# A two-layer trunk on one core: the odd mixer's output product, the down projections' product order and the opening's mean square rearranged

## The chip, the core and the metric

The kernel runs on one core of a Trainium2 chip. Its time is the device time of one execution in microseconds (us); the lower the better. Five engines work side by side and wait for each other by semaphores: TensorE (PE in the profile; its weight loads PEld), VectorE (DVE), ScalarE (ACT), GpSimd (POOL) and SyncE (SP), which issues transfers.

## The reference

```python
def reference(x, mem, ...):
    h = x
    for i in range(DEPTH):                       # DEPTH 2, SEQ 512, D_MODEL 1024, D_FF 2816
        f = swiglu_ffn(rms_norm(h, ffn1_pre_g[i]), ffn1_w_gu[i], ffn1_w_down[i])
        h = h + 0.5 * rms_norm(f, ffn1_post_g[i])
        hn = rms_norm(h, mix_pre_g[i])
        m = even_mixer(hn, ...) if i % 2 == 0 else odd_mixer(hn, ...)
        h = h + rms_norm(m, mix_post_g[i])
        c = memory_cross_attention(rms_norm(h, xa_pre_g[i]), mem, ...)
        h = h + rms_norm(c, xa_post_g[i])
        f = swiglu_ffn(rms_norm(h, ffn2_pre_g[i]), ffn2_w_gu[i], ffn2_w_down[i])
        h = h + 0.5 * rms_norm(f, ffn2_post_g[i])
    return h

def swiglu_ffn(h, w_gu, w_down):
    gate, up = jnp.split(h @ w_gu, 2, axis=-1)
    return (jax.nn.silu(gate) * up) @ w_down

def odd_mixer(h, w_in, w_group, scale, w_out):
    # p = h @ w_in, in 4 groups of 256 columns; group g: causal mean over WINDOWS[g] = (2, 4, 8, 16)[g]
    # positions, minus p; then (group @ w_group[g]) * scale, and the 1024 columns @ w_out
```

## The kernel before

The residual h stays in SBUF, 4 tiles of 128 positions. Every product is made of three matmuls (`mm3`): each operand is split into a high part (ScalarE casts it, line 72) and a low part (VectorE subtracts, line 73), and high by high, high by low and low by high are added up (lines 77, 78, 79). So an operand is ready only when ScalarE and then VectorE have had it; weights too (`whi`, `wlo`, made of a loaded `raw` tile), four of each kind, from seven `raw` tiles that SyncE fills (512 KB each). GpSimd issues transfers that add to what a tile holds already.

A feed-forward block works on its 2816 hidden columns in three parts (`FF_PARTS`). Up and gate of a part are made by `seven`, a scheme in which seven products of half-sized blocks take the place of eight; a product there is 24 matmuls of 256 columns. The hidden values are put into two tiles r, cut in four blocks: r11 and r12 are the left halves (positions 0 to 255), r21 and r22 the right halves. The down projection of the first two parts is made by `seven_tm`, again with seven products (24 matmuls of 512 columns each), in banks A, B and C of PSUM, whose operands are blocks and sums of blocks: a11 is r11, x1 is r21 - r22, x2 is x1 - r11, a12 is r12, x3 is r11 - r21, and so on; the weights are t1, b11, b21, b22, t3 and sums of them. The last half of r is written by line 580, after the last product of `seven`. There are 2 x 2 feed-forward blocks, so 8 passes through `seven_tm`; a first part (`fresh`) copies its results into f, a second part adds to them. The third part is made by `tm_last`, position tile by position tile, with the sandwich norm behind it: f is added (line 524), squared and summed on ScalarE (526), multiplied by the gain (532), m follows (533), GpSimd raises it to the power -1/2 (r, line 156), and line 536 adds to h.

The odd mixer makes its input projection, evacuates each group (`evac`), and VectorE makes the causal means (`pool`, lines 848 to 858). Then each group is multiplied by its weight matrix: two products of six matmuls (512 columns) to a group, evacuated by lines 891 (ScalarE, high) and 892 (VectorE, low). `tm_out` multiplies the result y by w_out: its first part (`head`) does four of eight blocks of rows of w_out, those of groups 3 and 2, for all four position tiles and the first 512 output columns, which is 4 x 4 x 3 = 48 matmuls and a quarter of the whole; then tile by tile the rest.

`rms_transpose` does a norm in front of a block: squares and sums on ScalarE (line 164), m on VectorE (166, 169), r on GpSimd, a scaled copy on ScalarE (173), and TensorE transposes it (180), from where VectorE (182) and `split` make the operands. In the opening this is done for the first two tiles before anything else, while the first weights land.

The tiles come from pools, and a scheduler decides by a model of costs and of free tiles in which order each engine gets its instructions; on each engine they then run in that order.

Of the kernel before, what the change touches and what calls it, by code (L numbers as in the profile page):

```python
# [10 lines left out]
P = 128  # L11
D = 1024
# [21 lines left out]
def trunk_kernel(tc, x, mem, ffn1_pre_g, ffn1_w_gu, ffn1_w_down, ffn1_post_g,  # L34
# [8 lines left out]
    with ExitStack() as es:  # L43
# [115 lines left out]
        def rms_transpose(src, g, x, t):  # L159
            xn = qt([P, D])  # L160
            ss = [small(1, "ss") for _ in range(2)]
            hs = [slice(0, 512), slice(512, 1024)]
            for i in range(2):
                nc.scalar.activation(out=xn[:, hs[i]], in_=src[:, hs[i]], func=AF.Square, accum_out=ss[i])
# [5 lines left out]
                                           op0=ALU.mult, op1=ALU.add)  # L170
            r = rsqrt(m2)
# [16 lines left out]
        class Prenorm:  # L188
# [12 lines left out]
            def tile(self, t):  # L201
                self.turns.append(rms_transpose(h[:, t, :], self.g, self.x, t))
# [131 lines left out]
        def seven_tm(w, k0, r, a11, f, fresh):  # L334
# [20 lines left out]
            b11 = load(0, 0)  # L355
            b22 = load(1, 1)
            b21 = load(1, 0)
            r11, r12, r21, r22 = r[0][:, :, :HALF], r[1][:, :, :HALF], r[0][:, :, HALF:], r[1][:, :, HALF:]

            def operand(src):  # L360
                o = ops4()
                split(o[:, 0], o[:, 1], src)
                return o
# [42 lines left out]
            a12 = operand(r12)  # L406
            u2 = product("A", t1, x2)
            t3 = load(0, 1)
            put(t3, 1, 1)
            put(t1, 1, 0)  # L410
            b22 = load(1, 1)
            take(0, 1, u2, None if fresh else "from")
# [8 lines left out]
            take(1, 0, product("A", t1, a22), None if fresh else add)  # L421
# [19 lines left out]
        def tm_out(a, w, k_order, post_g, nxt):  # L441
# [13 lines left out]
            for k in pairs[2:]:  # L455
                wk.update(w_pair(w, k, 0))
# [45 lines left out]
        def tm_last(a, wk, n, post_g, nxt, f):  # L502
# [3 lines left out]
            for t in range(NT):  # L506
# [12 lines left out]
                for c in range(2):  # L519
# [7 lines left out]
                    if c == 0:  # L527
# [29 lines left out]
        def ffn(pre, w_gu, w_down, post_g, nxt):  # L557
            f = []
            for j0, j1 in FF_PARTS:
# [3 lines left out]
                a11 = None  # L563
                for j in range(j0, j1, 2):
# [24 lines left out]
                    if not ending and j - j0 == 2:  # L589
                        a11 = ops4()  # L590
                        split(a11[:, 0], a11[:, 1], r[0][:, :, :HALF])
                n = j1 - j0
                if ending:
                    nx = nxt()
                    last_weights(w_down, j0, n, wk, False)
                    tm_last(hid, wk, n, post_g, nx, f)
                else:
                    seven_tm(w_down, j0, r, a11, f, not f)
# [223 lines left out]
        def odd(pre, l, o, post_g, nxt):  # L822
# [51 lines left out]
            for half in (1, 0):  # L874
# [4 lines left out]
                for g in (2 * half + 1, 2 * half):  # L879
                    if half == 0:  # L880
                        pool(g)
                    gi = g % 2
                    for j in range(2):
                        ps = psa()
                        for k in range(2):
# [7 lines left out]
                                                       op0=ALU.mult, op1=ALU.subtract)  # L893
            nx = nxt()
# [155 lines left out]
```

## Time and profile before

| | |
|---|---|
| three runs | 1979.59, 1980.74, 1982.03 us (median 1980.74) |
| profiled execution | 1980.61 us |
| span, first to last instruction | 1978.9 us |
| mean granted TensorE clock | 0.998 |
| TensorE busy | 1941.2 us, 98% |
| weight loads (beside the matmuls) | 1780.1 us, 90% |
| VectorE busy | 1480.1 us, 75% |
| ScalarE busy | 1036.0 us, 52% |
| GpSimd busy | 216.2 us, 11% |

The busy time of an engine is the time in which it ran an instruction; the profiled execution's own time is 1.7 us more than its span. The granted clock is 1.00 at 2.4 GHz and 0.50 at 1.2 GHz.

### The profile page before, as it was taken

Reading aid. Unit: us, or ns where it says so; the run is one execution under the profiler, and the core shown is the slowest. Engines: PE = TensorE matmul, PEld = TensorE weight load, DVE = VectorE, ACT = ScalarE, POOL = GpSimd, SP = SyncE. Lnnn points to the kernel's source line nnn. Section 1 sums busy time; section 2 is a strip of 40 time slices with the busy share of each in tenths; the row PEclk is TensorE's granted clock in tenths of the full one; section 3 lists DMA queues with packets and bytes.
Section 4 is the critical chain, followed back from the end, with each engine's and each line's share of the span. In section 5 each row is a group of like instructions: output and inputs, shape, how many; then the busy total and the mean of one; then the engine's idle time right before and its main releaser. Section 6 shows DMA issues by size and latency. Waiting matters only on the chain. (4 is left out here: it accounts for less than half of the span.)

```text
span 1978.9 us, 31832 instructions
## 1 busy us (share of the span) xinstructions
PE 1941.2 (98%) x12843; PEld 1780.1 (90%) x12843; DVE 1480.1 (75%) x1840; ACT 1036.0 (52%) x1477; POOL 216.2 (11%) x225
## 2 busy tenths in 40 slices
PE   7999999999999999999999999999999999999998
PEld 7989899888989889899998989899979889999897
DVE  6787877699956568877877786887766648776974
ACT  6555455544565455555455555455545545555462
POOL 1111110100010011111101111110001001111100
PEclk9999999999999999999999999999999999999999
DMA  7887884325845337888871787885234325887871
GB/s 203 223 213 185 202 206 154 109 86 181 280 143 185 86 75 182 213 181 203 212 214 43 203 206 190 201 211 173 75 107 147 98 57 129 208 215 199 203 184 43
DMA packets 251149, 327.76 MB, mean 166 GB/s; under 512 B 9854, under 2 KB 189654, under 8 KB 248954
## 3 DMA queue, kind: packets, MB, share of 16 engines
q1 hardware_dynamic: 193226, 241.80, 38.7%
q0 software_dynamic: 57600, 83.90, 23.3%
q8 instruction: 100, 1.64, 0.3%
q14 instruction: 47, 0.39, 0.1%
q10 hardware_dynamic: 176, 0.05, 0.0%
HBM read 315.22 MB, written 10.49 MB: 165 GB/s over the span
## 5 line engine op out<-in xcount | busy, mean ns | idle before, releaser
L77 PE MATMUL psa<-big,whi 128*128 128x256 f32 (+1 forms) x3056 | 883.1, 290 | 3.1 <-ACT big L72 3.1
L78 PE MATMUL psa<-big,whi 128*128 128x256 f32 (+1 forms) x3056 | 884.6, 290 | 0.5 <-DVE big L73 0.5
L79 PE MATMUL psa<-big,wlo 128*128 128x256 f32 (+1 forms) x3056 | 882.6, 289 | 0.5 <-DVE wlo L73 0.5
L72 ACT CAST whi<-raw 128x1024 fp32r<-128x1024 f32 x514 | 537.9, 1050 | 585.3 <-PE psa L78 260.0
L73 DVE TENSOR_TENSOR wlo<-raw,whi 128x1024 fp32r<-128x1024 f32 x514 | 625.3, 1224 | 238.5 <-ACT whi L72 235.8
L77 PEld LDWEIGHTS psa<-big,whi 128*128 128x128 f32 x3056 | 585.2, 192 | 12.1 <-ACT big L72 4.6
L78 PEld LDWEIGHTS psa<-big,whi 128*128 128x128 f32 x3056 | 586.0, 192 | 9.0 <-DVE big L73 1.4
L79 PEld LDWEIGHTS psa<-big,wlo 128*128 128x128 f32 x3056 | 585.5, 192 | 7.7 <-DVE wlo L73 0.7
L77 PE MATMUL psa<-whi,big 128*128 128x512 f32 x800 | 314.7, 393 | 7.7 <-ACT big L72 6.2
L78 PE MATMUL psa<-wlo,big 128*128 128x512 f32 x800 | 312.0, 390 | 0.0
L79 PE MATMUL psa<-whi,big 128*128 128x512 f32 x800 | 311.2, 392 | 0.4
L77 PEld LDWEIGHTS psa<-whi,big 128*128 128x128 f32 x800 | 150.6, 188 | 41.1 <-ACT big L72 9.5
L79 PEld LDWEIGHTS psa<-whi,big 128*128 128x128 f32 x800 | 150.3, 188 | 37.0 <-DVE big L73 5.6
L78 PEld LDWEIGHTS psa<-wlo,big 128*128 128x128 f32 x800 | 150.5, 188 | 30.1
L300 POOL DMA_DIRECT2D raw<-in_ffn_w_gu_dram x40 | 51.5, 1288 | 571.0 <-DMA raw<-in_ffn_w_gu_dram 428.0
L77 PE MATMUL psa<-big 128*128 128x512 f32 (+1 forms) x288 | 106.1, 370 | 0.8 <-ACT big L72 0.8
L78 PE MATMUL psa<-big 128*128 128x512 f32 (+1 forms) x288 | 105.7, 367 | 0.0
L156 POOL TENSOR_TENSOR r<-m,nhalf 128x1 f32<-128x1 f32 x74 | 47.0, 635 | 536.0 <-DVE m L533 184.7
L79 PE MATMUL psa<-big 128*128 128x512 f32 (+1 forms) x288 | 105.2, 366 | 0.0
L350 POOL DMA_DIRECT2D raw<-in_ffn_w_down_dram x48 | 57.5, 1225 | 261.6 <-DMA raw<-in_ffn_w_down_dram 155.2
L295 POOL DMA_DIRECT2D raw<-in_ffn_w_gu_dram x40 | 52.1, 1303 | 283.3 <-DVE big L73 148.4
L741 DVE SCALAR_TENSOR_TENSOR big<-big,par 128x511 f32<-128x511 f32 (+29 forms) x120 | 81.2, 743 | 0.0
(152 smaller groups left out, 1698.0 us busy)
## 6 DMA issues: line engine op xcount, KB each, us to landing
raw<-in_ffn_w_gu_dram SPq DMA_DIRECT2D x216, 512.0 KB, 4.7
raw<-in_ffn_w_down_dram SPq DMA_DIRECT2D x120, 512.0 KB, 4.2
raw<-in_ffn_w_gu_dram POOLq DMA_DIRECT2D x80, 512.0 KB, 8.1
raw<-in_ffn_w_down_dram POOLq DMA_DIRECT2D x48, 512.0 KB, 7.6
raw<-in_xa_w_kv_dram SPq DMA_DIRECT2D x32, 512.0 KB, 4.1
raw<-in_ev_w_in_dram SPq DMA_DIRECT2D x16, 512.0 KB, 5.3
kv<-big POOLq DMA_DIRECT2D x8, 1024.0 KB, 6.8
raw<-in_xa_w_q_dram SPq DMA_DIRECT2D x16, 512.0 KB, 3.4
```

The costliest lines, as they stand in the source:

```text
L72: nc.scalar.copy(out=hi, in_=src)
L73: nc.vector.tensor_tensor(out=lo, in0=src, in1=hi.bitcast(F32), op=ALU.subtract)
L77: nc.tensor.matmul(out=ps, lhsT=lhs[0], rhs=rhs[0], start=start, stop=skip, skip_group_check=skip)
L78: nc.tensor.matmul(out=ps, lhsT=lhs[0], rhs=rhs[1], start=False, stop=skip, skip_group_check=skip)
L79: nc.tensor.matmul(out=ps, lhsT=lhs[1], rhs=rhs[0], start=False, stop=stop or skip, skip_group_check=skip)
L156: nc.gpsimd.tensor_tensor(out=r, in0=m, in1=nhalf.broadcast_to([P, n]), op=ALU.pow)
L295: nc.gpsimd.dma_start(out=t1, in_=fm_rows(w, 0, ca), accum_op=ALU.add)
L300: nc.gpsimd.dma_start(out=t3, in_=fm_rows(w, 1, cb), accum_op=ALU.add)
L350: nc.gpsimd.dma_start(out=raws[kk], in_=rows(kh, kk, ch), accum_op=ALU.add)
L741: nc.vector.scalar_tensor_tensor(out=acc[:, c, s_:], in0=z[:, c, :SEQ - s_], scalar=par[:, c, CONV - 1 - s_:CONV - s_], in1=acc[:, c, s_:] ...
```

## The change

Four places are rearranged; the products computed are the same, but for the mean square of one tile, which is made from mean and variance.

1. The opening: the mean square of the second position tile is made by VectorE (`mean_square_stats`: two BN_STATS, one BN_AGGR, two small ones) and not by two squares on ScalarE.
2. `seven_tm`: the seven products stand in another order. The first two are p1 (a11) and the one with a12; then u2 (x2), q5 (x1), t3 (x3), and the last two as before. x3 and a11 are made in `ffn` after the second pair of hidden columns (`ready`), r11 - r21 is kept in r11's place, x2 is made from it in one instruction, b21 is loaded before b22, and the sum t1 + b22 goes into b11's tiles.
3. `tm_last`: the multiply by the gain is done by halves of the columns, and m and r stand in front of the second half's.
4. The odd mixer: the groups' products are cut in two (`grouped`). Groups 3 and 2 come first, then `tm_out` begins, and groups 1 and 0 follow behind its head.

```diff
+        def mean_square_stats(src, hs):
+            room = tp.tile([P, 512], F32, name="tmp", tag="tmp")
+            st = room[:, :12].rearrange("p (a b) -> p a b", a=2)
+            for i in range(2):
+                nc.vector.bn_stats(out=st[:, i, :], in_=src[:, hs[i]])
+            mv = room[:, 12:14]
+            nc.vector.bn_aggr(out=mv, in_=st)
+            m = small(1, "m")
+            nc.vector.tensor_scalar(out=m, in0=mv[:, 1:2], scalar1=EPS, scalar2=None, op0=ALU.add)
+            m2 = small(1, "m")
+            nc.vector.scalar_tensor_tensor(out=m2, in0=mv[:, 0:1], scalar=mv[:, 0:1], in1=m,
+                                           op0=ALU.mult, op1=ALU.add)
+            return m2
...
+            m2 = mean_square_stats(src, hs) if stats else mean_square(src, xn, hs)
...
             b11 = load(0, 0)
+            b21 = load(1, 0)
             b22 = load(1, 1)
-            b21 = load(1, 0)
...
-            e = qt([P, 4, HALF])
-            nc.vector.tensor_tensor(out=e, in0=r21, in1=r22, op=sub)
-            x1 = operand(e)
-            p1 = product("A", b11, a11)
+            a12 = operand(r12)
+            p1 = product("A", b11, ready[0])
...
-            nc.vector.tensor_tensor(out=e, in0=e, in1=r11, op=sub)
+            e = qt([P, 4, HALF])
+            nc.vector.scalar_tensor_tensor(out=e, in0=x3r, scalar=-1.0, in1=r22, op0=ALU.mult, op1=sub)
             x2 = operand(e)
+            take(0, 0, product("B", b21, a12), add)
+            for kk in range(2):
+                nc.vector.tensor_tensor(out=b11[kk], in0=t1[kk], in1=b22[kk], op=add)
+            nc.vector.tensor_tensor(out=r21, in0=r21, in1=r22, op=sub)
+            x1 = operand(r21)
+            u2 = product("A", b11, x2)
+            t3 = load(0, 1)
+            put(t3, 1, 1)
+            put(b11, 1, 0)
+            b22 = load(1, 1)
+            take(0, 1, u2, None if fresh else "from")
             q5 = product("C", t1, x1)
-            for kk in range(2):
-                nc.vector.tensor_tensor(out=t1[kk], in0=t1[kk], in1=b22[kk], op=add)
...
-            a12 = operand(r12)
-            u2 = product("A", t1, x2)
...
-            take(0, 0, product("B", b21, a12), add)
-            nc.vector.tensor_tensor(out=r11, in0=r11, in1=r21, op=sub)
-            x3 = operand(r11)
+            x3 = ready[1] if fresh else operand(x3r)
             take(1, 1, product("A", t3, x3), sub)
...
-            for k in pairs[2:]:
-                wk.update(w_pair(w, k, 0))
+            wk.update(w_pair(w, pairs[2], 0))
+            if mid:
+                mid()
+            wk.update(w_pair(w, pairs[3], 0))
...
-                m = small(1, "m")
-                nc.vector.tensor_tensor(out=ft, in0=ft, in1=gb, op=ALU.mult)
-                nc.vector.scalar_tensor_tensor(out=m, in0=ss[1], scalar=4.0 / D, in1=m0,
-                                               op0=ALU.mult, op1=ALU.add)
-                r = rsqrt(m)
+                    else:
+                        m = small(1, "m")
+                        nc.vector.scalar_tensor_tensor(out=m, in0=ss[1], scalar=4.0 / D, in1=m0,
+                                                       op0=ALU.mult, op1=ALU.add)
+                        r = rsqrt(m)
+                    nc.vector.tensor_tensor(out=ft[:, cs], in0=ft[:, cs], in1=gb[:, cs], op=ALU.mult)
...
                     if not ending and j - j0 == 2:
-                        a11 = ops4()
-                        split(a11[:, 0], a11[:, 1], r[0][:, :, :HALF])
+                        r11, r21 = r[0][:, :, :HALF], r[0][:, :, HALF:]
+                        ready = [operand(r11)]
+                        nc.vector.tensor_tensor(out=r11, in0=r11, in1=r21, op=ALU.subtract)
+                        if not f:
+                            ready.append(operand(r11))
...
-            for half in (1, 0):
+            def grouped(half):
...
+            grouped(1)
+            pool(1)
             nx = nxt()
-            tm_out(y, od_w_out[o], [6, 7, 4, 5, 2, 3, 0, 1], post_g, nx)
+            tm_out(y, od_w_out[o], [6, 7, 4, 5, 2, 3, 0, 1], post_g, nx, lambda: grouped(0))
...
-            pre.tile(t)
+            pre.tile(t, stats=t == 1)
```

Lines of the changed kernel have other numbers: 325, 327 and 580 become 344, 346 and 602; 402 becomes 421, the sum into b11; 417 and 422 make x2 and x1; 856 becomes 881; 891 and 892 become 916 and 917; 533 and 536 become 554 and 558.

VectorE at the first down part of the first block (the scheduler numbers the q tiles; in line 73 a `big` is an operand's low half, a `wlo` a weight's). Before:

```order
L325 TENSOR_TENSOR q_943<-q_943,psa 128x2x256
L73 TENSOR_TENSOR wlo<-raw,whi 128x1024
L327 TENSOR_TENSOR q_943<-psa,q_943 128x2x256
L580 TENSOR_TENSOR big<-q_942,q_943 128x2x256
L73 TENSOR_TENSOR wlo<-raw,whi 128x1024
L402 TENSOR_TENSOR raw<-raw 128x1024
L73 TENSOR_TENSOR wlo<-raw,whi 128x1024
L580 TENSOR_TENSOR big<-q_942,q_943 128x2x256
L402 TENSOR_TENSOR raw<-raw 128x1024
L392 TENSOR_TENSOR q_1170<-big 128x1024
L73 TENSOR_TENSOR wlo<-raw,whi 128x1024
L73 TENSOR_TENSOR big<-q_1170,big 128x1024
```

In the changed kernel:

```order
L421 TENSOR_TENSOR raw<-raw 128x1024
L344 TENSOR_TENSOR q_947<-q_947,psa 128x2x256
L73 TENSOR_TENSOR wlo<-raw,whi 128x1024
L346 TENSOR_TENSOR q_947<-psa,q_947 128x2x256
L602 TENSOR_TENSOR big<-q_946,q_947 128x2x256
L73 TENSOR_TENSOR wlo<-raw,whi 128x1024
L421 TENSOR_TENSOR raw<-raw 128x1024
L73 TENSOR_TENSOR big<-big 128x1024
L602 TENSOR_TENSOR big<-q_946,q_947 128x2x256
L73 TENSOR_TENSOR wlo<-raw,whi 128x1024
L417 SCALAR_TENSOR_TENSOR q_1214<-big 128x1024
L422 TENSOR_TENSOR big<-big 128x4x256
```

The last two sums of weights stood around the last hidden half (580), with x1's subtraction (392) behind them; now the first sum (421) stands in front of the third product's addition (344), a12's low half in front of the last hidden half (602), and x2 (417) and x1 (422) behind it.

TensorE in the odd mixer, from the end of groups 3 and 2 on: line 77 to 79 with `big` on the left are a group's product, those with `whi` or `wlo` on the left of `big` are the output product. Before:

```order
L79 MATMUL psa_14581<-big_14543,wlo_14549 128x512
L77 MATMUL psa_14607<-big_14604,whi_14592 128x512
L77 MATMUL psa_14618<-big_14604,whi_14592 128x512
L78 MATMUL psa_14607<-big_14604,whi_14592 128x512
...
L77 MATMUL psa_14636<-big_14633,whi_14592 128x512
L77 MATMUL psa_14645<-big_14633,whi_14592 128x512
L77 MATMUL psa_14657<-whi_14663,big_14559 128x512
L78 MATMUL psa_14657<-wlo_14664,big_14559 128x512
```

In the changed kernel:

```order
L79 MATMUL psa_14593<-big_14555,wlo_14561 128x512
L77 MATMUL psa_14616<-whi_14622,big_14571 128x512
L78 MATMUL psa_14616<-wlo_14623,big_14571 128x512
...
L79 MATMUL psa_14619<-whi_14628,big_14572 128x512
L77 MATMUL psa_14692<-big_14610,whi_14688 128x512
...
L79 MATMUL psa_14703<-big_14610,wlo_14689 128x512
L77 MATMUL psa_14616<-whi_14682,big_14699 128x512
...
L77 MATMUL psa_14721<-big_14718,whi_14688 128x512
```

Before, group 1 (big_14604) and group 0 (big_14633) follow on group 2, and the head (psa_14657 to 14660) begins among them; now the head's 48 matmuls (psa_14616 to 14619) stand between group 2 (psa_14593) and group 1 (psa_14692), and group 0 (psa_14721) comes after the first of what follows the head for tile 0.

VectorE over the same stretch: pool(0) is 848 to 856 before and 873 to 881 now, 892 or 917 evacuate groups' products. Before:

```order
L848 COPY big<-big 128x2
L849 TENSOR_TENSOR big<-big 128x2x511
L892 SCALAR_TENSOR_TENSOR big<-psa,cols,big 128x512 x2
L73 TENSOR_TENSOR big<-q_14596,big 128x1024
L892 SCALAR_TENSOR_TENSOR big<-psa,cols,big 128x512
L854 TENSOR_TENSOR big<-big,rec 128x2
L858 SCALAR_TENSOR_TENSOR big<-big 128x2x511
L892 SCALAR_TENSOR_TENSOR big<-psa,cols,big 128x512 x3
L856 TENSOR_TENSOR big<-big 128x2
L73 TENSOR_TENSOR wlo<-raw,whi 128x1024
L73 TENSOR_TENSOR big<-big 128x1024
```

In the changed kernel:

```order
L917 SCALAR_TENSOR_TENSOR big<-psa,cols,big 128x512 x2
L73 TENSOR_TENSOR big<-q_14602,big 128x1024
L917 SCALAR_TENSOR_TENSOR big<-psa,cols,big 128x512
L73 TENSOR_TENSOR wlo<-raw,whi 128x1024
L917 SCALAR_TENSOR_TENSOR big<-psa,cols,big 128x512
L879 TENSOR_TENSOR big<-big,rec 128x2
L883 SCALAR_TENSOR_TENSOR big<-big 128x2x511
L881 TENSOR_TENSOR big<-big 128x2
L73 TENSOR_TENSOR wlo<-raw,whi 128x1024 x2
L917 SCALAR_TENSOR_TENSOR big<-psa,cols,big 128x512
L73 TENSOR_TENSOR big<-big 128x1024
```

Before, three evacuations stand between 858 and 856 of pool(0); now the three last steps of pool(0) stand together, before the fifth evacuation.

## Rows read from the trace of the kernel before

**Rows 1.** What TensorE waits for, whole span: engine, tile, line, releaser, us, times, longest:
```profile
PE psa L77 <- ACT big L72: 10.1, 12, 2.7
PE tps L180 <- ACT q L173: 7.5, 5, 2.5
```

**Rows 2.** Timeline at the second product of a down part: start us, us, engine, line:
```profile
1719.93 1.22 DVE L402 TENSOR_TENSOR raw<-raw 128x1024 f32<-128x1024 f32 x1
...
1720.22 0.39 PE L79 MATMUL psa<-whi,big 128*128 128x512 f32 x1
...
1721.06 1.22 DVE L392 TENSOR_TENSOR q<-big 128x1024 f32<-128x1024 f32 x1
...
1722.26 0.39 PE L79 MATMUL psa<-whi,big 128*128 128x512 f32 x1
1722.32 1.05 ACT L72 CAST big<-q 128x1024 fp32r<-128x1024 f32 x1 [1.25 <-DVE q L392]
...
1723.41 0.50 PE L77 MATMUL psa<-whi,big 128*128 128x512 f32 x1 [0.77 <-ACT big L72]
...
1725.01 0.40 PE L77 MATMUL psa<-whi,big 128*128 128x512 f32 x1
```

**Rows 3.** What the results of line 392 are waited for by, us and times:
```profile
  ACT big L72: 10.0, 8
```

**Rows 4.** Timeline ahead of the same down part, VectorE and loads:
```profile
1707.96 6.12 SPq L345 DMA_DIRECT2D raw<-in_ffn_w_down_dram  x3
...
1711.53 0.69 DVE L325 TENSOR_TENSOR q<-q,psa 128x512 f32<-128x512 f32 x1 [0.72 <-PE psa L79]
...
1714.34 0.69 DVE L327 TENSOR_TENSOR q<-psa,q 128x512 f32<-128x512 f32 x1 [0.65 <-PE psa L79]
```

**Rows 5.** Loads of the page, last figure the median us from issue to landing:
```profile
raw<-in_ffn_w_down_dram SPq DMA_DIRECT2D x120, 512.0 KB, 4.2
```

**Rows 6.** Loads issued from 1670 to 1677 us, in the same form:
```profile
raw<-in_ffn_w_gu_dram SPq DMA_DIRECT2D x1, 512.0 KB, 6.5
```

**Rows 7.** Timeline of the odd mixer before its groups 0:
```profile
1456.22 1.22 DVE L858 SCALAR_TENSOR_TENSOR big<-big 128x1022 f32<-128x1022 f32 x1
...
1457.83 0.40 PE L79 MATMUL psa<-big,wlo 128*128 128x512 f32 x1
...
1458.98 0.75 DVE L892 SCALAR_TENSOR_TENSOR big<-psa,cols,big 128x512 fp32r<-128x512 f32 x1 [0.22 <-ACT big L891]
1459.65 0.15 DVE L856 TENSOR_TENSOR big<-big 128x2 f32<-128x2 f32 x1
...
1459.84 1.04 ACT L72 CAST big<-big 128x1024 fp32r<-128x1024 f32 x1 [0.89 <-DVE big L856]
...
1460.93 1.22 PE L77 MATMUL psa<-big,whi 128*128 128x512 f32 x2 [2.71 <-ACT big L72]
```

**Rows 8.** Busy time by engine of that stretch, granted clock, DMA share, GB/s:
```profile
1461.00:1464.40 3.40, 3.40 (x8) 2.72 (x9) 3.40 (x3) 1.77 (x2) 0.00 (x0) 0.51 0.49 157
```

**Rows 9.** Timeline of the opening:
```profile
8.45 1.33 ACT L173 ACTIVATE q<-h,r 128x512 f32<-128x512 f32 x2
...
12.05 1.34 ACT L173 ACTIVATE q<-h,r 128x512 f32<-128x512 f32 x2
...
12.83 3.08 PE L180 MATMUL tps<-ident,q 128*128 128x128 f32 x12 [2.50 <-ACT q L173]
...
17.29 0.39 PE L78 MATMUL psa<-big,whi 128*128 128x256 f32 x1 [0.53 <-DVE big L73]
```

**Rows 10.** Statistics instructions of the even mixer, ns min/median/max:
```profile
L679 DVE BATCH_NORM_STATS2 st<-big x4: 682/684/704, 434.0 to 443.8; 128x6 f32<-128x512 f32 x4
```

**Rows 11.** Timeline of the tail:
```profile
1971.87 1.23 DVE L532 TENSOR_TENSOR big<-big,post 128x1024 f32<-128x1024 f32 x1 [0.85 <-ACT sq L526]
1973.02 0.15 DVE L533 SCALAR_TENSOR_TENSOR m<-pss,m 128x1 f32<-128x1 f32 x1
...
1973.83 1.28 DVE L536 SCALAR_TENSOR_TENSOR h<-big,r,h 128x1024 f32<-128x1024 f32 x1 [0.66 <-POOL r L156]
```

More of the change, by code (lines that the diff above doesn't have):

```diff
@@ L157, in rsqrt, with mean_square @@
             return r
-        def rms_transpose(src, g, x, t):
-            xn = qt([P, D])
+        def mean_square(src, junk, hs):
             ss = [small(1, "ss") for _ in range(2)]
-            hs = [slice(0, 512), slice(512, 1024)]
             for i in range(2):
-                nc.scalar.activation(out=xn[:, hs[i]], in_=src[:, hs[i]], func=AF.Square, accum_out=ss[i])
+                nc.scalar.activation(out=junk[:, hs[i]], in_=src[:, hs[i]], func=AF.Square, accum_out=ss[i])
             m = small(1, "m")
@@ L170, in rms_transpose @@
                                            op0=ALU.mult, op1=ALU.add)
+            return m2
[11 more added lines that the diff above has]
+                                           op0=ALU.mult, op1=ALU.add)
+            return m2
+        def rms_transpose(src, g, x, t, stats=False):
+            xn = qt([P, D])
+            hs = [slice(0, 512), slice(512, 1024)]
+            m2 = mean_square_stats(src, hs) if stats else mean_square(src, xn, hs)
             r = rsqrt(m2)
@@ L199, in warm, with tile @@
                 self.ws = sum((w_fm(w, c0, raw) for c0, raw in zip(c0s, raws)), [])
-            def tile(self, t):
-                self.turns.append(rms_transpose(h[:, t, :], self.g, self.x, t))
+            def tile(self, t, stats=False):
+                self.turns.append(rms_transpose(h[:, t, :], self.g, self.x, t, stats))
             def turn_pair(self):
@@ L332, in seven, with operand, seven_tm @@
             done(out_a, out_b, product("A", b11, x.a22, False))
-        def seven_tm(w, k0, r, a11, f, fresh):
+        def operand(src):
+            o = ops4()
+            split(o[:, 0], o[:, 1], src)
+            return o
+        def seven_tm(w, k0, r, ready, f, fresh):
             def rows(kh, kk, ch):
@@ L355, in seven_tm @@
             b11 = load(0, 0)
+            b21 = load(1, 0)
             b22 = load(1, 1)
-            b21 = load(1, 0)
[L358 to L363, printed above, removed]
+            x3r, r12, r21, r22 = r[0][:, :, :HALF], r[1][:, :, :HALF], r[0][:, :, HALF:], r[1][:, :, HALF:]
             banks = {}
@@ L405, in seven_tm @@
             take(1, 1, q5, None if fresh else add)
-            a12 = operand(r12)
-            u2 = product("A", t1, x2)
[L408 to L412, printed above, removed]
-            take(0, 0, product("B", b21, a12), add)
-            nc.vector.tensor_tensor(out=r11, in0=r11, in1=r21, op=sub)
-            x3 = operand(r11)
+            x3 = ready[1] if fresh else operand(x3r)
             take(1, 1, product("A", t3, x3), sub)
@@ L420, in seven_tm @@
             take(0, 1, product("C", b22, x4), "from")
-            take(1, 0, product("A", t1, a22), None if fresh else add)
+            take(1, 0, product("A", b11, a22), None if fresh else add)
         def tm_part(accs, a, w, ks, first, last, ts=range(NT)):
@@ L439, in w_pair, with tm_out @@
             return {(c, k + i): (hi[:, i, :], lo[:, i, :]) for i in range(2)}
-        def tm_out(a, w, k_order, post_g, nxt):
+        def tm_out(a, w, k_order, post_g, nxt, mid=None):
             gb = gain(post_g, "post")
@@ L562, in ffn @@
                 r = None if ending else [big(F32), big(F32)]
-                a11 = None
+                ready = None
                 for j in range(j0, j1, 2):
@@ L597, in ffn @@
                 else:
-                    seven_tm(w_down, j0, r, a11, f, not f)
+                    seven_tm(w_down, j0, r, ready, f, not f)
             return nx
@@ L879, in odd @@
                 for g in (2 * half + 1, 2 * half):
-                    if half == 0:
+                    if g == 0:
                         pool(g)
```

## The prediction

> **What bounds the kernel now.** I read first the waits of TensorE, because TensorE works through nearly the whole span, so a change can only win where TensorE waits or runs at a lower clock. In that list the reader is to see that two kinds of wait hold nearly all: first matmuls that wait for the ScalarE cast of an operand (10.1 us in 12 waits), and transposes that wait for a scaled tile (7.5 us in 5) [rows 1]. Then I looked up where they stand, in the timeline. Eight of the twelve are the same place, the down projection of the first two parts of each feed-forward block (`seven_tm`, two parts in four blocks): VectorE's L392 is what the cast waits for, eight times [rows 3]. The longest one is in the odd mixer, 2.71 us [rows 7], and what follows it runs at a granted clock of 0.51 for 3.4 us [rows 8], which is the 1.2 GHz level. The longest transposes' waits lie in the opening [rows 9]. The tail behind the last matmul is a short chain on VectorE [rows 11].
>
> **The change, part by part.** The sum is made against the profiled execution, 1980.61 us (span 1978.9, and 1.7 around it); the median of the runs is 1980.74, so the two can be taken as one.
>
> *Down parts.* In one site the second product's first matmul should follow the last of p1 by one pitch, 0.227 us (1720.22 to 1722.26 is nine steps). It starts at 1723.41, and the sixth matmul after 1722.26 starts at 1725.01, since x1's low half is late too and the matmuls that want it are spread: 2.75 us for six steps that take 1.36, so 1.39 lost [rows 2]. Eight sites make 11.1. (These rows are from a first part. The profile has four sites of each kind.) The chain that is late is also there: the last half of the hidden tile, then L402, L392, ScalarE's cast from 1722.32 to 1723.37, in one line [rows 2]. The new order puts p1 and B in front, whose operands a11 and a12 come from halves of the hidden tiles that are done before the last one, and makes the first late operand (x2) wanted two products later. A product is 24 matmuls, 24 x 0.227 = 5.44 us, so p1 begins at 1722.26 + 0.23 - 5.44 = 1717.05 and u2 would begin at 1727.93, its first matmul on x2's low half two pitches later, 1728.38. What VectorE has to do after the last hidden half, which ends as L402 starts at 1719.93, by the new program order is at worst L421, a12's low half, one weight low half, L417, L422, another weight low half and x2's: seven at 1.13 (1719.93 to 1721.06), 7.9, so 1727.8: in time by 0.5. In a second part two additions into the output (of L325's kind, 0.69 each [rows 4]) stand between them as well: 1729.2, late by 0.8, at four sites 3.3. At best L421 and a12's half lie ahead of 1719.32, and it is in time everywhere. ScalarE has one cast for each of these operands and is not full there. t3 and the last b11 are loaded, and added to by GpSimd's queue, no later than today, as each waits for a weight tile that is now used no later.
>
> There is one new danger. The first L421 (b11 = t1 + b22) now stands on VectorE in front of L344, the read of bank A that the last `seven` product waits for. L344 is today's L325, at 1711.53; the last product can start when the one before it ends, which the start of L327 shows, 1714.34 [rows 4]. b22 is now loaded after b21, so its first half goes out where b21's does today, at 1707.96 [rows 4], and at the 4.2 us that such a load takes [rows 5] it lands at 1712.2. L421 may begin at 1714.34 - 0.69 - 1.13 = 1712.5 at the latest. So it fits by 0.3 at the median load and doesn't if it takes over 4.5. One load of that size on this queue took 6.5 [rows 6]. I charge 0.1 a site, 0.8 in all, for this and for x2 together. **Term: -10.3; between -5.5 (0.7 lost again at each site) and -11.1**, or -12 if the second parts lose a little more today than the site that I read.
>
> That a late instruction holds up ready ones behind it is what the odd mixer's rows show: L892 at 1458.98 had waited 0.22 for ScalarE, and L856 behind it, whose input was written by L858 (1456.22, 1.22 long), starts at 1459.65 [rows 7]. The Trainium skill (Perfetto Trace Analysis, section Tensor Engine Instruction) says the same of these queues, "ACT/DVE/GPSIMD are strict FIFO". By that rule a late b22 reaches TensorE in full, and the trace agrees.
>
> *Odd mixer.* Today pool(0)'s last step L856 stands behind the evacuations of group 1 on VectorE, ScalarE casts its result at 1459.84, and TensorE, done at 1457.83 with what it could do, starts group 0 at 1460.93: 3.10 less one pitch is 2.87 lost [rows 7]. Half clock for 3.4 us [rows 8] loses 1.7 more. The change puts 48 head matmuls (10.9 us at 0.227) in front of groups 1 and 0. VectorE's work until pool(0) is ready is the same, so with 10.9 us of cover against 2.87 missing it is ready long before. What is late next: the first output matmuls of columns that group 1 and 0 make. Each group product is six matmuls, 1.36, and its evacuation 0.69 on ScalarE and 0.75 on VectorE, of which the first output matmul needs the first and its third the second; counted through, each is in time by 0.2 to 0.4. I leave 0.2 for it. SP's second group load goes behind two output loads, wanted 10.9 us later than before. **Term: -4.4, between -1 and -4.6.**
>
> *Opening.* The second tile's squares leave ScalarE, so its scaling starts where the first tile's ends, 8.45 + 1.33 = 9.78, instead of 12.05: 2.27 earlier [rows 9]. VectorE takes two BN_STATS (0.68 each [rows 10]) and an aggregate instead, ahead of the first weight's low half, where it has little else to do. The transposes' wait of 2.50 shrinks by it. But TensorE waits again, at 17.29, for a low half from VectorE [rows 9], which must come earlier as well, and two later tiles are scaled after that. Of 2.27 I take two thirds, **-1.5, between -0.5 and -2.5** (the whole wait).
>
> *Last part.* m and r no longer stand behind the multiply by the gain. In the tail L533 follows the 1.23 us of L532, 1973.02 against 1971.87, and the last L536 waits for r [rows 11]. So h comes 1.15 earlier: one half of the multiply is done before the last matmul, the other fits between m and h, which are 0.81 apart. **-1.1, between -0.9 and -1.15.** The other fifteen ends of this form have no wait of TensorE that I can price; 0, between +0.5 (0.15 more of VectorE each, if some count) and -0.9.
>
> **Sum:** 10.3 + 4.4 + 1.5 + 1.1 = 17.3, and 1980.6 - 17.3 = **1963.3**.
>
> **The rivals.**
> 1. *The wait moves to b22 or x2* (VectorE's order, above). For it: both margins are some tenths. Against: with a load of median length both are in time. With 0.7 lost a site, 5.6 less the 0.8 charged: 1968.1.
> 2. *The odd mixer pays again.* Four of six banks now hold the output's sums, so the four group products take turns in two, and a bank is free only after 0.69 + 0.75. For it: the two evacuations (1.44) are longer than the next product (1.36). Against: output matmuls can stand between. If a gap near 2.7 comes back, the half clock does too, and the term is gone: 1967.7.
> 3. *The new order brings the down parts nothing*, as x2 is as late as x1 was. For it: it has the same chain of subtraction, cast and subtraction. Against: 10.9 us of products ahead of it instead of 5.4. 1973.6.
> 4. *Slower:* b22's landing alone. Each 0.1 us beyond 4.5 us costs 0.8 over eight sites. All 17.3 are gone at 2.2 a site, a landing of 6.7 us from the issue at every one of them, and over 0.2% is lost from 2.7 on. The 6.5 [rows 6] shows that it can come near; that it was the one such load in its window, against a median of 4.2 [rows 5], speaks against it. At 2.7 a site: 1984.9, before any loss of clock, which by the odd mixer's rows would add up to 1.7 a site.
>
> **How the numbers follow.** The forecast has 0.68, rival 1 0.14, rival 2 0.09, rival 3 0.05, rival 4 0.04 (half of it within 0.2%, half beyond). 0.2%, 4 us, is about what a measurement of this kernel can tell from no change. Faster: 0.96 less a rest for what I haven't seen, 0.95; same 0.02; slower 0.03. The range: all upper ends (12 + 4.6 + 2.5 + 1.15 + 0.9 = 21.2) give 1959.5; the upper end takes in rivals 1 and 2 and, in part, both together, 1970. Rivals 3 and 4 and the tails stay outside.
>
> **What would show it.** In the changed profile the eight waits before the down parts' products are gone from TensorE's list, with nothing over 0.2 at L344's reader; if the first L421 ends past 1714 in the corresponding site, rival 1 or 4 is at work. In the odd mixer there is no gap over 0.6 and the granted clock stays at 1.00 behind the groups. In the opening the second set of transposes starts near 10.5. At the end m is made in front of the second half's multiply, not behind it. What would make it wrong: waits of some tenths at many places that the new order makes and that no row of today's shows.

## The result, and the profile after

The changed kernel takes 1960.49 us (median of 4 runs, 1959.48 to 1961.9) beside 1981.38 (4 runs, 1979.59 to 1982.2): a ratio of 0.9897, interval 0.9886 to 0.9909. It is faster by 20.9 us, 2.8 us below the predicted 1963.3 and inside the range. The profiled execution is the one of 1959.48 us, with a span of 1956.7, 22.2 less than before.

TensorE's waits, whole span, in the form of [rows 1]:
```profile
PE tps L199 <- ACT q L192: 6.0, 4, 2.0
PE psa L77 <- ACT big L72: 1.9, 5, 0.4
PE psa L78 <- DVE big L73: 0.8, 1, 0.8
```
The waits for a cast have gone from 10.1 us in 12 to 1.9 in 5, none over 0.4. The transposes' waits have lost 1.5.

VectorE ahead of a down part, beside [rows 4] (L421 is the sum t1 + b22, L344 reads the bank), and the first matmul of the last `seven` product, which fills that bank again:
```profile
1692.95 1.23 DVE L421 TENSOR_TENSOR raw<-raw 128x1024 f32<-128x1024 f32 x1 [0.47 <-DMA raw<-in_ffn_w_down_dram]
1694.09 0.68 DVE L344 TENSOR_TENSOR q<-q,psa 128x512 f32<-128x512 f32 x1
...
1695.81 0.28 PE L77 MATMUL psa<-big,whi 128*128 128x256 f32 x1
```
What VectorE waits for before its sixteen instructions of L421 (us, times):
```profile
  DMA raw<-in_ffn_w_down_dram: 5.2, 8
```
So the new wait exists: VectorE idles for b22 at all eight sites, 0.65 us on average. But L344 ends at 1694.77 here and TensorE wants the bank at 1695.81, 1.04 to spare where I had 0.3. Over the eight sites it is 0.32 to 1.04, so TensorE doesn't see the wait.

The odd mixer, one window from the groups to the output's matmuls, in the form of [rows 8] (PE, weight loads, VectorE, ScalarE, GpSimd, then granted clock):
```profile
1430.00:1465.00 35.00, 35.00 (x154) 28.41 (x154) 22.02 (x28) 17.23 (x22) 0.00 (x0) 1.00 0.39 120
```
The profile has TensorE busy for all 35 us at the 2.4 GHz level; three of its steps there are longer than a pitch by 0.11 or 0.12 us. The 2.71 of [rows 7] and the 0.51 of [rows 8] are gone.

TensorE in the opening, beside [rows 9]:
```profile
9.32 4.27 PE L199 MATMUL tps<-ident,q 128*128 128x128 f32 x16 [2.02 <-ACT q L192]
...
14.49 0.39 PE L78 MATMUL psa<-big,whi 128*128 128x256 f32 x1 [0.79 <-DVE big L73]
14.71 0.28 PE L79 MATMUL psa<-big,wlo 128*128 128x256 f32 x1
14.83 0.28 PE L77 MATMUL psa<-big,whi 128*128 128x256 f32 x1
```
The sixteen transposes run in one go. The L78 that waits for a low half starts at 14.49 instead of 17.29, and matmuls of 256 columns follow each other by 0.12.

The tail, beside [rows 11]:
```profile
1950.42 0.16 DVE L554 SCALAR_TENSOR_TENSOR m<-pss,m 128x1 f32<-128x1 f32 x1 [0.85 <-ACT sq L547]
1950.50 0.68 DVE L557 TENSOR_TENSOR big<-big,post 128x512 f32<-128x512 f32 x1
1950.66 0.93 POOL L156 TENSOR_TENSOR r<-m,nhalf 128x1 f32<-128x1 f32 x1 [7.23 <-DVE m L554]
1951.62 1.29 DVE L558 SCALAR_TENSOR_TENSOR h<-big,r,h 128x1024 f32<-128x1024 f32 x1 [0.44 <-POOL r L156]
```
m comes first, and h still waits for r, 1.20 behind m instead of 0.81.

**Where the 22.2 us came from.** I took every matmul of the two traces and summed by stage how much later the next one starts than one pitch (0.227 us for 512 columns, 0.120 for 256, 0.109 for a transpose):

| stage | lost before | lost after | difference |
|---|---|---|---|
| the eight down sites | 12.5 | 0 | 12.5 |
| odd mixer | 4.8 | 0.4 | 4.5 |
| opening, first 40 us | 5.95 | 3.9 | 2.05 |
| even mixer, 460 to 490 us | 2.7 | 0.75 | 1.95 |
| all other stages | 13.0 | 12.5 | 0.5 |
| last matmul to end of span | 8.95 | 8.22 | 0.73 |

The even mixer's code is unchanged; its 1.95 is taken up below.

### The profile page after: what moved, and what is told of

Its sections match the earlier page's. It is cut to its first block, busy times and chain, and to the rows that moved or that the text cites. A ratio compares the mean times of both kernels' runs of the same rounds, so it can differ in the third digit from the quotient of the medians.

```text
span 1956.7 us, 31900 instructions
## 1 busy us (share of the span) xinstructions
PE 1931.5 (99%) x12843; PEld 1780.0 (91%) x12843; DVE 1476.3 (75%) x1859; ACT 1035.9 (53%) x1473; POOL 220.6 (11%) x225
## 5 line engine op out<-in xcount | busy, mean ns | idle before, releaser
L78 PE MATMUL psa<-big,whi 128*128 128x256 f32 (+1 forms) x3056 | 883.9, 289 | 0.8 <-DVE big L73 0.8
L72 ACT CAST whi<-raw 128x1024 fp32r<-128x1024 f32 x514 | 537.9, 1050 | 554.7 <-PE psa L78 251.1
L78 PEld LDWEIGHTS psa<-big,whi 128*128 128x128 f32 x3056 | 585.7, 192 | 8.7 <-DVE big L73 1.0
L78 PE MATMUL psa<-wlo,big 128*128 128x512 f32 x800 | 311.3, 389 | 0.0
L78 PEld LDWEIGHTS psa<-wlo,big 128*128 128x128 f32 x800 | 150.3, 188 | 30.1
L78 PE MATMUL psa<-big 128*128 128x512 f32 (+1 forms) x288 | 105.7, 367 | 0.0
L72 ACT CAST big<-big 128x1024 fp32r<-128x1024 f32 (+1 forms) x78 | 65.8, 852 | 38.4 <-PE psa L79 20.0
```

The lines of the kernel that those rows point to most:

```text
L72: nc.scalar.copy(out=hi, in_=src)
L78: nc.tensor.matmul(out=ps, lhsT=lhs[0], rhs=rhs[1], start=False, stop=skip, skip_group_check=skip)
```

## The experiments

My theory was the prediction's: the four terms add up, each where it was put. The rivals were that the wait moves to b22 or x2, and that the odd mixer pays again. Times are medians beside the kernel before on the same chip. That kernel gave 1980.13 in the batch of the first four (25 runs, 1977.81 to 1984.63), 1979.86, 1981.82 and 1980.68 in the later ones. The changed kernel was timed with the result only, so a difference from its 1960.49 also holds a difference between chips, which the ratios to the kernel before leave out.

**One part alone on the kernel before.** Four kernels, each with one of the four numbered items of the change and nothing else.

*The down parts (item 2).*
```diff
...
-        def seven_tm(w, k0, r, a11, f, fresh):
+        def seven_tm(w, k0, r, ready, f, fresh):
...
+            take(0, 0, product("B", b21, a12), add)
...
+            u2 = product("A", b11, x2)
...
             q5 = product("C", t1, x1)
...
```


> The kernel before with the down parts' new order alone. Theory (each part takes away the loss of its own stage, and no more): the eight waits before the second products go, and with them what the spread low halves and the second parts' further 0.3 us cost, 12.5 us in the changed kernel's trace: 1968.5. The prediction's own term, with 0.8 charged for the sum behind b22, would be 1970.3. Rival (the order brings new waits that the other parts hide or cure): 6 or less gained, over 1974. The even mixer's gap of 1.57 us before the gated half, where no line was changed, is there again if a part other than this one removed it, or gone if the landing of the memory tile decides it by itself.

Measured: 1967.96 (ratio 0.9933, 0.992 to 0.9945), 12.2 less. Its waits of TensorE for a cast:
```profile
PE psa L77 <- ACT big L72: 4.0, 4, 2.7
```
The eight are gone; the longest left is the odd mixer's. The new order alone brings, within the interval, the whole loss of the eight sites.

*The odd mixer (item 4).*
```diff
...
-            for half in (1, 0):
+            def grouped(half):
...
+            grouped(1)
+            pool(1)
...
-            tm_out(y, od_w_out[o], [6, 7, 4, 5, 2, 3, 0, 1], post_g, nx)
+            tm_out(y, od_w_out[o], [6, 7, 4, 5, 2, 3, 0, 1], post_g, nx, lambda: grouped(0))
```


> The kernel before with the odd mixer's order alone. Theory: the gap of 2.71 us and the 3.4 us of half clock go, and the 0.25 ahead of them, 4.8 together: 1976.2; the prediction's term was 4.4. Rival (the odd mixer pays again, by its two rotating banks): under 1 gained, 1980, with a gap of over 1 us among the groups' products.

Measured: 1976.67 (0.9978, 0.9969 to 0.9988), 3.5 less. No wait of TensorE between 1440 and 1480. This execution has half clock at another place, the seam into the second feed-forward block (timeline, then windows):
```profile
731.47 1.32 PE L180 MATMUL tps<-ident,q 128*128 128x128 f32 x8 [1.69 <-ACT q L173]
```
```profile
732.60:735.90 3.30, 3.30 (x18) 3.30 (x17) 3.29 (x6) 1.73 (x3) 0.00 (x0) 0.50 0.64 104
```
Nothing of that seam was edited; together with the wait it loses 3.7 us here, where it loses 2.1 in the kernel before.

*The opening (item 1).*
```diff
...
-            pre.tile(t)
+            pre.tile(t, stats=t == 1)
```


> The kernel before with the opening's mean square alone. Theory: 2.1 us gained as in the trace of the changed kernel, 1978.9; the prediction's term was 1.5, between 0.5 and 2.5. Rival (the part of the opening that is won is lost again at the next tiles' scaling): 0.5 or less. The first matmul on a low half starts near 14.5 us, not at 17.3.

Measured: 1977.22 (0.9981, 0.9972 to 0.999), 2.9 less, more than my 1.5.

*The last part (item 3).*
```diff
-                nc.vector.tensor_tensor(out=ft, in0=ft, in1=gb, op=ALU.mult)
...
+                    nc.vector.tensor_tensor(out=ft[:, cs], in0=ft[:, cs], in1=gb[:, cs], op=ALU.mult)
...
```


> The kernel before with the last parts' halves alone. Theory: the tail is 0.7 shorter, as in the changed kernel, where r took 0.93 us on GpSimd beside VectorE's multiply and not 0.55; with the other fifteen ends within 0.5 of nothing: 1980, not to be told from the kernel before. The prediction's term was 1.1. Rival (the last part also moves the even mixer's VectorE ahead of TensorE): the gap of 1.57 us there is gone and 2 us more are gained, 1978.

Measured: 1979.55 (0.9993, 0.9985 to 1.0002), 0.6 less, which the timing alone can't tell from nothing. From the last matmul to the last tile's first output transfer it is 4.48 instead of 5.23. Alone, the four make 12.2 + 3.5 + 2.9 + 0.6 = 19.2. Together they made 20.9 against the four runs of the kernel before that stand with the result, but 19.6 against the 25 runs that the parts are taken from: that the parts fall short of the whole is not shown.

**b22 late.** The changed kernel with b22's loads issued by GpSimd.
```diff
...
-            b22 = load(1, 1)
+            b22 = load(1, 1, nc.gpsimd)
```


> The changed kernel, with b22's two loads on GpSimd's queue instead of SyncE's; all else, VectorE's order too, stays. It makes the prediction's fourth rival true on purpose. Theory (VectorE runs in order, so the sum 421 that waits for b22 holds up 344, and with it the last product before each down part): in the changed kernel 421 begins at 1692.95, 344 ends at 1694.78, and its bank is wanted at 1696.0, a margin of 1.2. GpSimd's accumulating loads take 7.6 us in the page where SyncE's take 4.2; a b22 that comes 3.4 later or more than it does costs 2.2 to 3.1 a site, 18 to 25 over eight: 1978 to 1985, and more if the clock falls behind such gaps. Rival (other ready work passes the waiting sum, or the landing has slack): no change from 1960.5.

Measured: 1962.84 (0.9915, 0.9901 to 0.9928). My dose was wrong: I took the 7.6 us of the adding transfers of this queue, and a plain load landed 3.74 after its issue (median of 16, 3.66 to 5.19), about 0.5 more than the 3.2 or so of SyncE's. VectorE at the site with the longest wait, and what TensorE waited for there:
```profile
796.92 1.23 DVE L421 TENSOR_TENSOR raw<-raw 128x1024 f32<-128x1024 f32 x1 [1.76 <-DMA raw<-in_ffn_w_down_dram]
798.06 0.68 DVE L344 TENSOR_TENSOR q<-q,psa 128x512 f32<-128x512 f32 x1
```
```profile
PE psa L77 <- DVE q L344: 0.2, 1, 0.2
```
The mechanism of rivals 1 and 4 is there (L344 behind a waiting L421, TensorE behind L344): VectorE waits 1.2 to 1.8 us for b22 at the eight sites, six keep 0.2 to 0.3 us of their margin, and at two TensorE starts the last product 0.3 and 0.1 late. So what is left in the changed kernel is small: a wait that is 0.7 us longer on average uses most of it up. The profiled execution has a span 4.4 us longer than the changed kernel's, of which 1.9 lie in the opening and 1.8 in the even mixer; where the 2.3 between the medians lies is not shown.

**b22 early.** The changed kernel with b22 in front of b21 again.
```diff
-            b21 = load(1, 0)
             b22 = load(1, 1)
+            b21 = load(1, 0)
```


> The changed kernel, with b22 loaded before b21 again. b22's first half then leaves where b21's does, some 6 us earlier, and both sums stand earlier on VectorE. Theory (the sum behind b22 has a margin of about 1.1 us in the changed kernel at every site, so the landing costs nothing): no change from 1960.5 within 0.2%, no wait of TensorE at the down parts. Rival (the 0.8 us charged for that margin are really lost somewhere): 1959.7 or less. Rival (b21, now the later load, is wanted by the second product): waits for b21's high half at eight sites, over 1 us each, 1968 or more.

Measured: 1958.3 (0.9884, 0.9868 to 0.9901). No wait before the down parts' products either, and the margin at L344 is 1.47 at every site. Its interval overlaps that of the changed kernel; 2 us less is a hint. A part of it can be seen in the traces, at a place that nobody meant to change, the transposes behind the odd mixer near 1500 us. In the changed kernel r on GpSimd starts just behind a low half of VectorE there:
```profile
1499.94 0.69 DVE L73 TENSOR_TENSOR big<-tmp,big 128x512 fp32r<-128x512 f32 x1
1500.02 1.04 POOL L156 TENSOR_TENSOR r<-m,nhalf 128x1 f32<-128x1 f32 x1 [3.38 <-DMA raw<-in_xa_w_o_dram]
...
1501.86 0.33 PE L199 MATMUL tps<-ident,q 128*128 128x128 f32 x1 [0.98 <-ACT q L192]
```
With b22 early it starts ahead of it:
```profile
1501.83 0.56 POOL L156 TENSOR_TENSOR r<-m,nhalf 128x1 f32<-128x1 f32 x1 [3.05 <-DMA raw<-in_xa_w_o_dram]
1502.09 0.69 DVE L73 TENSOR_TENSOR big<-tmp,big 128x512 fp32r<-128x512 f32 x1 [0.35 <-ACT big L72]
...
1503.20 0.33 PE L199 MATMUL tps<-ident,q 128*128 128x128 f32 x1 [0.17 <-ACT q L192]
```
This stage loses 1.2 us in the changed kernel and 0.45 with b22 early, as in the kernel before.

**Half the cover.** The groups 1 and 0 go behind the first 24 of the 48 head matmuls.
```diff
             for k in head:
+                if mid and k == head[2]:
+                    mid()
...
-            if mid:
-                mid()
```


> The changed kernel, with groups 1 and 0 behind the first 24 matmuls of the output product's head (5.4 us) instead of behind all 48. Theory (the cover must only exceed the 2.87 us that were missing): no gap over 0.5 before group 0, no half clock there, 1960.5 as the changed kernel. Rival (a good part of the 10.9 us is used up, since VectorE gets the evacuations of four banks in between): a gap of 1 or more and a time of 1962 to 1965.

Measured: 1959.76 (0.9899, 0.9885 to 0.9912). The window over the groups:
```profile
1425.00:1465.00 40.00, 40.00 (x178) 32.98 (x177) 31.00 (x41) 20.48 (x26) 0.00 (x0) 1.00 0.40 124
```
5.4 us of cover do what 10.9 do.

**No cover.** The groups go in front of all head matmuls.
```diff
+            if mid:
+                mid()
             for k in head:
...
-            if mid:
-                mid()
```


> The changed kernel, with groups 1 and 0 in front of the head again, so that only pool(1)'s place and the two functions' form are left of the odd mixer's change. Theory (the cover is what does it): the gap of 2.7 before group 0 and the half clock of 3.4 us behind it are back, 4.5 more than the changed kernel: 1965.0. Rival (what does it is that pool(0)'s last steps no longer stand behind evacuations): half the gap or less, and 1962 or less.

Measured: 1964.85 (0.9922, 0.9909 to 0.9936), 4.4 over the changed kernel and 5.1 over the one with half the cover, which ran on the same chip. Timeline and window:
```profile
1448.41 1.22 PE L77 MATMUL psa<-big,whi 128*128 128x512 f32 x2 [2.71 <-ACT big L72]
```
```profile
1448.20:1451.60 3.40, 3.19 (x8) 2.51 (x9) 3.40 (x4) 2.05 (x3) 0.00 (x0) 0.51 0.50 154
```
The gap of [rows 7] and the clock of [rows 8] are back to the digit. The expectation's rival is not ruled out by it, because VectorE's order came back too, with three evacuations (L917) again between the last two steps of pool(0):
```profile
1443.68 1.22 DVE L883 SCALAR_TENSOR_TENSOR big<-big 128x1022 f32<-128x1022 f32 x1
1444.82 1.41 DVE L917 SCALAR_TENSOR_TENSOR big<-psa,cols,big 128x512 fp32r<-128x512 f32 x2
1446.46 0.75 DVE L917 SCALAR_TENSOR_TENSOR big<-psa,cols,big 128x512 fp32r<-128x512 f32 x1 [0.23 <-ACT big L916]
1447.12 0.15 DVE L881 TENSOR_TENSOR big<-big 128x2 f32<-128x2 f32 x1
```
They take 2.3 of the 2.71 us, so a cover of 10.9 us and the better order of VectorE would each go far, and this run takes both away. The kernel with half the cover tells more: there one evacuation stands between, L881 ends at 1447.21, and a cast of 1.05 behind it gives 1448.3, while group 0 would be wanted at 1446.8 if the 24 head matmuls did not stand ahead (an estimate: TensorE is done at 1444.06, and group 1 is twelve steps of 0.227). So about 1.5 us are hidden by the cover itself.

**The gain apart.** In all last parts the product with the gain goes to tiles of its own, ahead of m, and h is made by halves.
```diff
+                    nc.vector.tensor_tensor(out=fg[c], in0=ft[:, cs], in1=gb[:, cs], op=ALU.mult)
...
-                    nc.vector.tensor_tensor(out=ft[:, cs], in0=ft[:, cs], in1=gb[:, cs], op=ALU.mult)
...
```


> The changed kernel, with the gain's product of the last part written to tiles of its own, so that VectorE makes it while ScalarE squares, and nothing of VectorE runs beside GpSimd's power; h is then written by halves. Theory (GpSimd's power takes 0.93 us beside VectorE's multiply and 0.55 alone): r takes 0.55 in the tail, and the way from the last matmul to the last transfer's issue is 4.1 to 4.2 instead of 4.48, 0.3 less; the whole 1960, not to be told from the changed kernel. Rival (0.93 was chance): r 0.55 to 0.93 whatever runs beside it, no shorter tail.

Measured: 1960.52 (0.9902, 0.9889 to 0.9916). The tail's timeline:
```profile
1954.36 0.16 DVE L557 SCALAR_TENSOR_TENSOR m<-pss,m 128x1 f32<-128x1 f32 x1
1954.60 0.55 POOL L156 TENSOR_TENSOR r<-m,nhalf 128x1 f32<-128x1 f32 x1 [7.61 <-DVE m L557]
1955.18 1.42 DVE L562 SCALAR_TENSOR_TENSOR h<-tmp,r,h 128x512 f32<-128x512 f32 x2 [0.66 <-POOL r L156]
```
With no multiply beside it, r takes 0.55 and h follows m by 0.82. The last tile's first transfer goes out 3.57 behind the last matmul instead of 4.48. But two inner seams lose over 1 us more each (near 350 and 1390 us, 0.8 in the changed kernel, 1.9 and 2.0 now). The one near 1500 us loses 0.5 instead of 1.2, and nothing is left in the median.

**The gain apart in the final block alone.**
```diff
+                apart = isinstance(nxt, Finish)
...
```


> The changed kernel, with the gain's product in tiles of its own in the very last part alone, where e9_gain_apart shortened the tail by 0.91 us while it lost some 1.1 each at three seams. Theory: tail 3.57 instead of 4.48 us, seams as in the changed kernel, 0.9 gained: 1959.6, which the measurement can hardly tell from the changed kernel. Rival (the seams' loss comes from the other feed-forward ends by chance): seams as in e9_gain_apart, 1960.5 or more.

Measured: 1959.36 (0.989, 0.9876 to 0.9905), with the tail at 3.57 and the seams near 350, 1050, 1390 and 1500 us as in the changed kernel; there were two losing seams in the run before this one, not three. 1.1 less, inside the interval.

**Both hints together.** b22 early, and the gain apart in the final block.


> The changed kernel with e10_old_loads' order of loads and e11_tail_apart's tail. Theory (the tail's 0.9 us is real; the loads' order changes nothing, and e10's 1958.3 is the opening's and the even mixer's luck): 1959.4, with a spread like e11's. Rival (the old order of loads is better by 2 us by itself): 1957.4.

Measured: 1958.59 (0.9888, 0.9871 to 0.9904), no better than b22 early alone. That both add up is not shown. 1958.3 and 1958.59 are the lowest medians here, some 2 us below the changed kernel.

**The memory tile.** The changed kernel with the second memory tile of the even mixer loaded from GpSimd's queue.
```diff
-                nc.sync.dma_start(out=mm, in_=mem[0, t * P:(t + 1) * P, :])
+                (nc.gpsimd if t else nc.sync).dma_start(out=mm, in_=mem[0, t * P:(t + 1) * P, :])
```


> The changed kernel, with the second memory tile loaded by GpSimd's queue instead of SyncE's, in the even mixer. Theory (VectorE's instruction 638 waits for that tile, the convolutions stand behind it, and the wait in front of the gated half follows from it: waits of 0.8 to 2.75 us gave losses of 0.5 to 1.74): GpSimd's plain load lands in 3.7 us, VectorE does not wait at 638, and the loss near 475 us is 0.3 or less, where the other runs of the changed kernel had 0.5 to 1.74; 1959.5. Rival (the tile lands late because the transfers are full, on whichever queue): the wait stays at 1 or more, and the loss at 1 to 1.7.

Measured: 1960.89 over three executions (0.99, 0.9884 to 0.9917). A fourth took 3182.89 us, at a mean granted clock of 0.557; it is like no other of any kernel and is not explained. VectorE's wait at the even mixer, in the kernel before, the changed one and this one:
```profile
DVE m L613 <- ACT q L611: 2.8, 1, 2.8
```
```profile
DVE m L638 <- ACT q L636: 0.8, 1, 0.8
```
```profile
DVE m L638 <- ACT q L636: 3.1, 1, 3.1
```
The tile landed 7.4 us after its issue; in the changed kernel the squares that need it begin 6.1 after the issue on SyncE's queue, in the kernel before 7.8. Another queue didn't bring it sooner. The DMA share around it is 0.84 in the kernel before, 0.92 in the changed one and 0.74 here, so that full transfers make it late is not shown.

## Why the prediction was right, point by point

**Down parts: the mechanism right, the term too small** (-10.3; 12.2 less alone, 12.5 in the trace). Two sizes were off. I charged 0.8 for the margins of b22 and x2, and nothing was lost: at the site that corresponds to [rows 4] the load took about 3.2 us instead of 4.2, which left 1.04 instead of 0.3. (I had read the moment at which the bank is wanted from VectorE's L327, 1714.34; the matmul itself starts at 1714.13, so the 0.3 was 0.1.) And I scaled a first part's 1.39 to all eight sites; counted over the trace, first parts lost about 1.4 and second parts 1.7. The case of my bound of -12, "if the second parts lose a little more", was the true one. Rival 1 was wrong by its margin, not by its mechanism: the smallest margin is 0.32, and the kernel with b22 late shows it used up.

**Odd mixer: right** (-4.4; 4.5 in the trace, 4.4 to 5.1 lost again with the groups in front of the head, 3.5 alone). I had put all of it down to the cover; VectorE's order changed with it, and how much of the 2.87 is due to which is shown only in part. Rival 2 fell: no step there loses more than 0.12 us with two free banks. That the output matmuls between the group products are the reason, as I had set against it, was not tested by itself.

**Opening: the term too small** (-1.5; 2.05 between the two profiles, 2.9 alone, interval 2.0 to 5.5). The step that failed is the "two thirds": of the 2.27 about nine tenths arrived, 2.07 by the start of the 700th matmul, and the low half from VectorE came earlier by 2.8 (14.49 against 17.29). The size differs between executions, as matmuls reach the fast pace at different times. In the down parts' kernel, whose opening is that of before, they still follow each other by 0.21 at 17.7 us, and by 0.12 from 22.4 on:
```profile
17.72 0.42 PE L79 MATMUL psa<-big,wlo 128*128 128x256 f32 x1
17.94 0.42 PE L77 MATMUL psa<-big,whi 128*128 128x256 f32 x1
...
22.42 0.28 PE L78 MATMUL psa<-big,whi 128*128 128x256 f32 x1
22.54 0.28 PE L79 MATMUL psa<-big,wlo 128*128 128x256 f32 x1
```
Of the old openings, one profile reached it at 17.1 and three near 22; of the new ones, five near 13 and five near 18.5. Like with like, by the start of the 700th matmul: 98.84 old and 96.7 to 96.8 new where it came early, 2.1 less; 100.8 to 101.1 old and 98.2 to 98.8 new where it came late, 2.5 less. An old late one and a new early one are 4.0 to 4.4 us apart, an old early one and a new late one 0.1 to 0.7, so a part of the 2.9 may be the pace. A window ahead of the fast pace prints a granted clock of 1.00, but that is no reading: the trace's record of the clock begins only there, at 1.00, at 17.08 us in the kernel before, at 22.40 in the down parts' kernel and at 13.42 in the changed one. By the matmuls, the slow pace is that of 1.2 GHz: 0.213 us for 256 columns here, 0.427 for 512 in the half-clock stretch of [rows 8]. The Trainium skill says of that clock's default state that it is throttled and "activity releases the throttle" (TensorE: Matmul & The Clock Gate, section What's actually happening). The trace agrees as far as the pace and the start of the record go; why the rise comes at different times no run shows.

**Last part: half right** (-1.1; 0.73 in the tail, 0.6 alone). The order came as foreseen, and m was ahead of the second half's multiply. The step that failed is "the other fits between m and h, which are 0.81 apart". It fits on VectorE, but r on GpSimd took 0.93 beside it and 0.55 without it, and both kernels with the gain apart have the 0.55 back. The Trainium skill has it (SBUF — State Buffer, section Who interferes with whom): an instruction of VectorE with two inputs in SBUF contends with one of GpSimd that reads SBUF. The trace agrees, in that r ends at 1951.59, 0.41 behind the multiply's end, and not 0.55 behind its own start. So do all 14 profiles, with 74 such r each. Where a VectorE instruction with two inputs in SBUF was running as r started, r took 0.65 us or more, 283 times of 283; where such an instruction began only while r ran, r took under 0.6, 134 times of 134. I hadn't weighed it.

**What I didn't foresee: the even mixer.** No line of its code was changed, but TensorE's wait for a low half of VectorE is shorter there. Before and after:
```profile
PE psa L77 <- DVE big L73: 1.6, 1, 1.6
```
```profile
PE psa L77 <- DVE big L73: 0.3, 1, 0.3
```
VectorE's m waits for the squares of the second memory tile, and those for its landing; the convolutions that feed that low half stand behind m. The wait of m was 2.8 us before and 0.8 after, and from 0.41 to 3.11 over the other profiles, and in all 14 the stage from 460 to 490 us lost as much as m had waited, within 0.12 us (0.4 to 3.0). So the loss follows that wait, and it makes about 2 of the 22.2 between the two profiles. What sets the landing stays open. Chance of the transfers is one reading; but the four profiles without the down parts' new order lost 2.0 to 2.7, and the nine that have it and load the tile as before 0.4 to 2.5, so that the change itself brings the tile sooner is not excluded. How much of the medians' difference it carries stays open too.

## What to carry to other kernels

Where an operand is late at every pass, look for products whose operands are finished earlier and put them in front; the cover has to exceed the gap, and more brings nothing (5.4 and 10.9 us against 2.87). A price measured at one site is counted over all sites before it is multiplied. A small instruction on GpSimd that sits on the critical chain is timed with what VectorE is running when it starts, not from its time alone.

## What the runs showed of the hardware

- The wait of TensorE of 2.7 us before group 0 stands in five profiles, and in all five some 3.4 us at the 1.2 GHz level follow. A wait of 1.7 to 1.8 us at the seam near 725 us was followed by it in four profiles, which lost 3.7 to 3.9 us there; in the ten others, with waits of 1.2 to 2.1 us, it stayed away, and they lost 1.7 to 2.6. The kernel before spreads over 6.8 us in 25 runs; that this is a cause was not tested.
- A plain load of 512 KB from GpSimd's queue landed in 3.74 us (median of 16) at the down parts, where the profile's row for that queue and source, whose transfers add to their target, has a median of 7.6.
- GpSimd's power of 128x1 takes 0.55 us (median of 74), and 0.65 to 1.54 where a VectorE instruction with two inputs in SBUF is running as it starts (283 of 1036 in the 14 profiles; 0.93 in the tail). One that begins after it leaves it at 0.55. Another 32 took near 1.09 with no VectorE instruction beside them; what held those up is not known.
